# Between the last attention heads and the output projection: one store for both parts of a head's output, the last half's norm one part sooner, scratch cut per 256 tokens, and the products that are ready first put first

## The chip, the cores and the metric

The kernel runs on one core of one Trainium2 chip. A core has a matrix engine (TensorE, "PE" in the profile, with its weight loads as "PEld"), a vector engine (VectorE, "DVE"), a scalar engine (ScalarE, "ACT"), a third elementwise engine (GpSimd, "POOL"), and SyncE ("SP"), which here issues all transfers between the on-chip memory and device memory. Each engine takes its instructions in program order and waits on semaphores of the others. The metric is the device time of one execution in microseconds.

## What is computed

Two layers of a decoder over 1024 tokens of width 1024, in float32. The part that matters here is each layer's attention and the output projection behind it:

```python
# layer 0: 8 FoX heads and 8 MLA heads of width 64, their outputs side by side
m = jnp.concatenate([fox_out, mla_out], axis=-1) @ w_out      # 1024 x 1024
# layer 1: 8 differential heads of width 128, each normed over its width
o = _rms_norm(o, subln) * (1.0 - lambda_init)
m = o.reshape(bsz, seq, ODD_MIX_WIDTH) @ w_out
# both layers
x = x + _rms_norm(m, norm_mix_post[layer])
h = _rms_norm(x, norm_ffn_pre[layer])
f = _conv_ffn(h, ffn_w_up[layer], ffn_conv_w[layer], ffn_conv_b[layer], ffn_w_down[layer])
x = x + _rms_norm(f, norm_ffn_post[layer])
```

## The kernel before

**Products.** Every float32 product is made of three matrix products: a value is split into a high part `h`, rounded to the format that PE reads, and a low part `l = x - h`; `mm3` (L143) issues high x high, high x low and low x high into one PSUM bank. So each operand is made twice on the elementwise engines: ACT casts the high part and DVE or POOL subtracts (`split`, L121 and L122).

**Order.** The kernel is written in a tile framework that puts the instructions of each engine in order by a simulated timeline, and gives out buffers by tag: `Q` and `WL` hold 2 KB per partition each, `o` has two buffers, `h` and `l` one each (the tiles `oso`, `osh`, `osl`). Whatever changes a wait or a buffer can move instructions anywhere in the stages around it. Generators are woven: the scores and pv products of a head are mixed with dense products (weights, the first half of the output projection).

**Heads of layer 0.** A head goes through four parts of 256 query rows, j = 3, 2, 1, 0. `p_transpose` turns the probabilities (PE L385, then the cast to `pt`/`ptq` on ACT L389 and the subtraction on DVE L390). `pv64` multiplies them with V, whose high and low parts stand side by side in 128 columns, so that rows 0 to 63 and 64 to 127 of the bank `pspv` are to be added: ACT copies one half to `o` (L412), DVE adds the other (L413), ACT casts `h` (L414), POOL subtracts `l` (L415), and SP stores both to the scratch `oT` in device memory (L417, L418). It runs 64 times.

**Heads of layer 1.** `diff_head` makes parts of 256 rows too, and norms halves of 512 rows, i.e. two parts. `sub_a` squares a half (ACT L1175), sums the squares on PE (L1177) and takes the reciprocal root on DVE, sixteen small operations of 128 x 4 one behind the other (L172 to L179, then L1182 and L1183). `sub_b` spreads the result over the rows through diagonal matrices (L1192, L1193, PE L1195 and L1196), scales (DVE L1198), splits and stores (L1202, L1203), for c = 0 and 1, 256 tokens each. Both are put in a list (`pend`) and called one part later each: half 1, complete after j = 2, has its `sub_a` called at j = 1 and its `sub_b` at j = 0.

**Output projection.** `out_first` multiplies heads 0 to 3 (k 0 to 3) into the first 512 columns while the heads still run. `out_second` does the rest for blocks of 128 tokens, m = 7 down to 0: `ot` is the transposed head output, loaded by `oT_load` from the scratch (SP L442), kg = 0 for k 0 to 3 and kg = 1 for k 4 to 7. For each m, bank `psS` gets k 4 to 7 of the first 512 columns (n = 0, 12 matmuls) and bank `psmm` all eight k of the last 512 (n = 1, 24 matmuls). What follows an m on DVE, ACT and POOL is the post-norm, the residual sum and the pre-norm of the feed-forward part; SP also loads the residual rows `xr` (L198).

## Time and profile before

| | us |
|---|---|
| three runs, median | 2580.59 |
| lowest and highest of them | 2574.98, 2582.19 |
| the profiled execution, its own time | 2578.5 |
| its span, first to last instruction | 2576.4 |

The mean granted clock of TensorE in it is 0.977. The page gives for each engine its busy time, the share of the span and the number of instructions; a row of a timeline gives start, duration, engine, line, operation, output and inputs, shape, count, and in brackets the idle time before it with what ended that. The names are those of the program. The stages that the change touches lie in the profile as follows.

| stage | us from the span's start |
|---|---|
| layer 0, heads | about 110 to 564 |
| layer 0, first product of `out_second` behind the heads | 570.6 |
| layer 1, last product of the last head's part 2 | 1814.7 |
| layer 1, first product of `out_second` behind the heads | 1831.1 |

### The profile page before, as it was taken

The page shows a single profiled execution, that of the slowest core. Times are in us where ns is not written, and L with a number is a line of the kernel's source. Part 1 is how long each engine was busy: PE and PEld are TensorE (multiplying, and loading weights), DVE is VectorE, ACT ScalarE, POOL GpSimd, SP SyncE. Part 2 cuts the span into 40 slices and gives each one's busy share as a digit, 9 for nine tenths or more (in the row PEclk, how much of TensorE's full clock was granted, in tenths as well). Part 3 has the DMA queues.
Part 4 walks back from the last instruction along what each step waited for, and adds up shares of the span by engine and source line. Part 5 has one row for each costly group of instructions (what it writes and reads, how often), then busy time and mean ns, then how long its engine had stood idle before and what let it go on. Part 6 is the DMA issues. An engine that isn't in the chain of part 4 may idle for free.

```text
span 2576.4 us, 36603 instructions
## 1 busy us (share of the span) xinstructions
PE 2457.8 (95%) x12326; PEld 2072.2 (80%) x12326; DVE 1754.5 (68%) x3615; ACT 1232.3 (48%) x2457; POOL 1256.7 (49%) x1140
## 2 busy tenths in 40 slices
PE   9999899989899999989999999999889999999898
PEld 7888788868688888868888888888768888887786
DVE  5556788758766665666876777678687656656668
ACT  4455578654433333434545555456453333334353
POOL 3445665444577777740421323222257777776122
PEclk9999999999899999999999999999899999999899
DMA  3232333355223323584432213133732332328545
GB/s 142 86 99 80 105 90 88 105 163 189 73 94 112 109 93 112 182 276 151 164 136 58 70 49 88 34 107 107 237 115 88 105 106 98 107 102 278 169 150 192
DMA packets 189531, 316.16 MB, mean 123 GB/s; under 512 B 17928, under 2 KB 85144, under 8 KB 189344
## 3 DMA queue, kind: packets, MB, share of 16 engines
q1 hardware_dynamic: 189344, 313.83, 37.5%
q8 instruction: 98, 1.61, 0.3%
q14 instruction: 89, 0.73, 0.1%
HBM read 222.23 MB, written 76.85 MB: 116 GB/s over the span
## 4 chain that ended last, share of the span: by engine, by line
PE 38%; DVE 5%; DMA 2%; POOL 2%; issue 2%; ACT 1%; SPq 0%; DVEq 0%; POOLq 0%; ACTq 0%
PE psmm L143 19%; PE psS L143 6%; PE pstr L143 6%; PE pspv L143 5%; PE pstr L385 1%; DVE d L122 1%; DMA wdside<-in_ffn_down_dram 0%; DMA dB<-in_ffn_down_dram 0%; PE pstr L1177 0%; POOL d L122 0%; DVE xq L222 0%; DVE t L348 0%; DVE dT L726 0%; DVE xq L221 0%; DVE t L1230 0%
## 5 line engine op out<-in xcount | busy, mean ns | idle before, releaser
L143 PE MATMUL psmm<-hT,whi 128*128 128x512 f32 (+1 forms) x960 | 309.9, 399 | 2.3 <-DVE qb L320 2.3
L356 ACT ACTIVATE t<-t,mn 128x896 f32<-128x896 f32 (+7 forms) x256 | 198.8, 777 | 126.1 <-DVE mn L348 114.8
L122 POOL TENSOR_TENSOR wlo<-wraw,whi 128x512 fp32r<-128x512 f32 (+2 forms) x96 | 129.5, 1358 | 260.0 <-ACT whi L121 234.9
L122 POOL TENSOR_TENSOR d<-uraw,d 128x512 fp32r<-128x512 f32 x66 | 103.8, 1593 | 215.5 <-ACT d L121 209.5
L143 PEld LDWEIGHTS psmm<-hT,whi 128*128 128x128 f32 (+1 forms) x960 | 174.0, 188 | 35.9 <-issue 2.5
L143 PE MATMUL psmm<-hT,wlo 128*128 128x512 f32 (+1 forms) x480 | 189.4, 395 | 0.8 <-POOL wlo L122 0.8
L121 ACT CAST d<-uraw 128x512 fp32r<-128x512 f32 x154 | 91.8, 618 | 139.8 <-DMA uraw<-uS 67.9
L385 PE MATMUL pstr<-ident,t 128*128 128x128 f32 x864 | 136.4, 281 | 7.6 <-DVE t L1230 3.1
L143 PE MATMUL psmm<-whi,hT 128*128 128x256 f32 (+1 forms) x576 | 123.6, 303 | 5.4 <-DVE hT L253 2.8
L143 PE MATMUL psmm<-wo,ot 128*128 128x512 f32 x448 | 123.7, 396 | 0.0
L385 PEld LDWEIGHTS pstr<-ident,t 128*128 128x128 f32 x864 | 103.5, 145 | 17.9 <-DVE t L1230 3.7
L630 ACT ACTIVATE y<-y,cols 128x1024 f32<-128x1024 f32 x44 | 50.7, 1152 | 138.4 <-DVE y L628 138.4
L143 PE MATMUL pstr<-T,S3h 128*128 128x512 f32 x352 | 112.1, 399 | 3.8 <-DVE B L523 3.8
L626 ACT ACTIVATE y<-gate,cols 128x1024 f32<-128x1024 f32 x44 | 50.8, 1155 | 130.7 <-DVE gate L621 130.7
L143 PE MATMUL psmm<-B,A12h 128*128 128x512 f32 x352 | 109.0, 390 | 2.1 <-DVE B L523 2.1
L143 PE MATMUL psmm<-B,A11h 128*128 128x512 f32 x352 | 109.4, 390 | 0.0
L143 PE MATMUL pstr<-T,A22h 128*128 128x512 f32 x352 | 108.7, 389 | 0.0
L143 PE MATMUL psmm<-T,S2h 128*128 128x512 f32 x352 | 108.4, 389 | 0.0
L122 DVE TENSOR_TENSOR S2l<-s,S2h 128x512 fp32r<-128x512 f32 x44 | 56.7, 1289 | 74.8 <-ACT S2h L121 74.8
L143 PEld LDWEIGHTS psmm<-hT,wlo 128*128 128x128 f32 (+1 forms) x480 | 90.1, 188 | 20.8 <-POOL wlo L122 1.0
L390 DVE TENSOR_TENSOR ptq<-pstr,ptq 128x512 fp32r<-128x512 f32 (+1 forms) x160 | 99.4, 629 | 10.3 <-ACT ptq L389 7.9
L143 PE MATMUL psS<-B,S4h 128*128 128x512 f32 x336 | 103.7, 390 | 1.1 <-ACT S4h L121 1.1
(362 smaller groups left out, 7540.5 us busy)
## 6 DMA issues: line engine op xcount, KB each, us to landing
ot<-oT SPq DMA_DIRECT2D x96, 256.0 KB, 3.8
wg<-in_ffn_up_dram SPq DMA_DIRECT2D x44, 512.0 KB, 3.5
wv<-in_ffn_up_dram SPq DMA_DIRECT2D x44, 512.0 KB, 3.5
uS<-us SPq DMA_DIRECT2D x88, 256.0 KB, 2.0
uraw<-uS SPq DMA_DIRECT2D x40, 512.0 KB, 4.1
uA<-y SPq DMA_DIRECT2D x66, 256.0 KB, 2.1
wdside<-in_ffn_down_dram SPq DMA_DIRECT2D x66, 256.0 KB, 4.8
uraw<-uA SPq DMA_DIRECT2D x30, 512.0 KB, 4.3
```

The lines of the kernel that those rows point to most:

```text
L121: nc.scalar.copy(R(hi), raw)
L122: return lo_eng.tensor_tensor(R(lo), raw, hi, ALU.subtract).ins
L143: ins = nc.tensor.matmul(out, R(l), R(r), start=first and j == 0, stop=last and j == n - 1, skip_group_check=more).ins
L356: nc.scalar.activation(t[:, :W], t[:, :W], AF.Exp, bias=mn, scale=-1.0, accum_out=l)
L385: nc.tensor.transpose(tp[:, c:c + P], pts[qi][:, b * P:(b + 1) * P], ident)
L390: nc.vector.tensor_tensor(R(pl[:, :c]), tp[:, :c], ph[:, :c], ALU.subtract)
L626: nc.scalar.activation(y, gp, AF.Copy, scale=col(2, f))
L630: nc.scalar.activation(y, y, AF.Gelu_apprx_tanh, bias=cb)
```

## The change

There are five edits. (1) The scratch `oT_d` is cut into one tile for each layer, kg and part j, so that a load waits for the stores of its own 256 tokens and heads. (2) `pv64` always puts its sum in partitions 0 to 63, writes the high part to partitions 0 to 63 and the low part to 64 to 127 of one buffer, and stores both with one transfer; the buffer alternates between the tags `h` and `l`; the subtraction is an operation of DVE (`scalar_tensor_tensor`) in place of POOL's. (3) In `out_second`, the load for m = 7 of kg = 0 takes its buffers from `WL`; m = 7 and m = 6 do n = 1 before n = 0, and m = 6 begins n = 1 with k 0 to 3, as m = 7 did already. (4) `sub_b` does c = 1 first and leaves the low part where the sum stood, in `osub`. (5) For the last head, `sub_a` of half 1 is called as soon as part j = 2 is done, which brings its `sub_b` to j = 1.

```diff
@@ -111,7 +111,8 @@
     kr_d = dr.tile([2, 32, S], F32, tag="kr_d", name="kr_d")
     cr_d = dr.tile([2, S], F32, tag="cr_d", name="cr_d")
     ck_d = dr.tile([8, S], F32, tag="ck_d", name="ck_d")
-    oT_d = [dr.tile([2, 8, P, S], F32, tag=f"oT{i}", name=f"oT{i}") for i in range(2)]
+
+    oT_d = [[[dr.tile([2, 4, P, 256], F32, tag=f"oT{i}{kg}{j}", name=f"oT{i}{kg}{j}") for j in range(4)] for kg in range(2)] for i in range(2)]
     u_d = [{n: dr.tile([NP, P, HALF], F32, tag=f"u{n}{i}", name=f"u{n}{i}") for n in ("A11", "A12", "A22", "S1", "S2", "S3", "S4")}
            for i in range(2)]
 
@@ -395,6 +396,8 @@
             out.append((b, ph[:, c0:c0 + n], pl[:, c0:c0 + n], qi * P))
         return out
 
+    stg = [0]
+
     def pv64(pts, i0, vcols, up, oT, k, done):
 
         ov = bank("pv", 256)
@@ -405,17 +408,15 @@
                 done += (256 - c0) / 9216
             if kb + 2 < nb:
                 yield done
-        a0, b0 = (64, 0) if up else (0, 64)
+
         o = ostage("o", bufs=2)
-        h, l = ostage("h"), ostage("l")
-        ra, rb = slice(a0, a0 + 64), slice(b0, b0 + 64)
-        nc.scalar.copy(o[ra], ov[rb])
-        nc.vector.tensor_tensor(o[ra], ov[ra], o[ra], ALU.add)
-        nc.scalar.copy(R(h[ra]), o[ra])
-        nc.gpsimd.tensor_tensor(R(l[ra]), o[ra], h[ra], ALU.subtract)
-        qs = slice(i0 * P, i0 * P + 256)
-        nc.sync.dma_start(oT[0, k, ra, qs], h[ra])
-        nc.sync.dma_start(oT[1, k, ra, qs], l[ra])
+        stg[0] ^= 1
+        hl_ = ostage("hl"[stg[0]])
+        nc.scalar.copy(o[0:64], ov[64:128])
+        nc.vector.tensor_tensor(o[0:64], ov[0:64], o[0:64], ALU.add)
+        nc.scalar.copy(R(hl_[0:64]), o[0:64])
+        nc.vector.scalar_tensor_tensor(R(hl_[64:128]), o[0:64], 1.0, hl_[0:64], ALU.mult, ALU.subtract)
+        nc.sync.dma_start(oT[k // 4][i0 // 2][:, k % 4, 64 * up:64 * up + 64, :], hl_)
         yield done
         return done
 
@@ -440,7 +441,7 @@
         for j in range(2):
             t = buf(tag, "ot")
             nc.sync.dma_start(t.rearrange("p (k c) -> p k c", k=4),
-                              oT[j, 4 * kg:4 * kg + 4, :, m * P:(m + 1) * P].rearrange("k p c -> p k c"))
+                              oT[kg][m // 2][j, :, :, (m % 2) * P:(m % 2 + 1) * P].rearrange("k p c -> p k c"))
             ts.append(t)
         return ts
 
@@ -469,7 +470,7 @@
 
         lo = buf("X", "wo")
         w1 = wo_load(w_src, 0, 1, lambda k: (buf("Q", "woh"), lo[:, k, :]))
-        o1 = {7: oT_load(oT, 0, 7, "Q")}
+        o1 = {7: oT_load(oT, 0, 7)}
         w0 = wo_load(w_src, 4, 0, lambda k: (buf("Q", "woh"), buf("Q", "wol")))
         w1 += wo_quads(w_src, 4, 1)
         ot = {m: oT_load(oT, 1, m) for m in (7, 6, 5)}
@@ -482,10 +483,10 @@
                 o1[m - 1] = oT_load(oT, 0, m - 1, "Q")
             if m:
                 fin_0(m - 1)
-            rows = []
-            for n in range(2):
+            rows = {}
+            for n in (1, 0) if m > 5 else (0, 1):
                 o = bank("S" if n == 0 else "mm")
-                ks = ((4, 5, 6, 7) if n == 0 else (0, 1, 2, 3, 4, 5, 6, 7) if m == 7 else (4, 5, 6, 7, 0, 1, 2, 3))
+                ks = ((4, 5, 6, 7) if n == 0 else (0, 1, 2, 3, 4, 5, 6, 7) if m > 5 else (4, 5, 6, 7, 0, 1, 2, 3))
                 for k in ks:
                     src = (ot if k > 3 else o1)[m]
                     mm3(o, hl(tuple(t[:, (k % 4) * P:(k % 4 + 1) * P] for t in src), w0[k - 4] if n == 0 else w1[k]), k == ks[0], k == ks[-1])
@@ -495,7 +496,7 @@
                     fin_e(m, 0, r)
                 else:
                     r = o
-                rows.append(r)
+                rows[n] = r
             fin_a(m, 1, rows[1], rows[0])
             if m < 7:
                 fin_b(m + 1)
@@ -1185,7 +1186,7 @@
 
     def sub_b(h, half, o, rh, rl):
         eng = nc.vector if h == 7 and LV else nc.gpsimd
-        for c in range(2):
+        for c in (1, 0):
             dh, dl = ostage("h"), ostage("l")
             for m in range(2):
                 ms, mc = slice(m * P, (m + 1) * P), slice(2 * c + m, 2 * c + m + 1)
@@ -1196,11 +1197,11 @@
             nc.tensor.matmul(rb, ones_r, R(dl), start=False, stop=True)
             oc = o[:, c * 256:(c + 1) * 256]
             nc.vector.scalar_tensor_tensor(oc, oc, subg, rb, ALU.mult, ALU.mult)
-            oh, ol = ostage("o", bufs=2), ostage("o", bufs=2)
-            split(oc, oh, ol, eng)
-            qs = slice(half * HALF + c * 256, half * HALF + (c + 1) * 256)
-            nc.sync.dma_start(oT_d[1][0, h, :, qs], oh)
-            nc.sync.dma_start(oT_d[1][1, h, :, qs], ol)
+            oh = ostage("o", bufs=2)
+            split(oc, oh, oc, eng)
+            od = oT_d[1][h // 4][2 * half + c]
+            nc.sync.dma_start(od[0, h % 4], oh)
+            nc.sync.dma_start(od[1, h % 4], oc)
 
     def diff_head(h, maps, V, pend):
 
@@ -1247,6 +1248,8 @@
             nc.scalar.copy(o[:, (j % 2) * 256:(j % 2 + 1) * 256], ov)
             if j % 2 == 0:
                 pend.append(lambda h=h, j=j, o=o, l1=l1: sub_a(h, j // 2, o, l1))
+                if h == 7 and j == 2:
+                    pend.append(pend.pop(0)())
             yield done
 
     values, maps = diff_v(0, VT), diff_qk(0)
```

Lines of the changed kernel are higher by one from L115 on, by three from L400 on until `pv64`'s end and by one behind it (L143 is L144, L442 is L443, L1195 is L1196). Three places show how the order of the instructions moves.

PE at the end of layer 0's heads, before the change. `pspv` is the bank of a part of the last head, `ot_7039` the high part of heads 4 to 7 for m = 7:

```order
L143 MATMUL pspv_6903<-ptq_713,Vm_4308 128x256 x2
L143 MATMUL pspv_6903<-ptq_713,Vm_4308 128x128 x2
L143 MATMUL pspv_6958<-ptq_713,Vm_4308 128x256 x2
L143 MATMUL pspv_6958<-ptq_713,Vm_4308 128x128 x2
L143 MATMUL psS_7065<-woh_7007,ot_7039 128x512
L143 MATMUL psS_7065<-wol_7008,ot_7039 128x512
L143 MATMUL psmm_7082<-wo_7025,ot_7039 128x512
```

So PE goes from the last pv (`pspv_6958`, part 0) straight to k 4 to 7 of m = 7. With the change, PE ahead of the last head's first pv; `ot_6937` and `ot_6939` are the high and low parts of heads 0 to 3 for m = 6:

```order
L386 MATMUL pstr_6676<-ident,t_6606 128x128
L386 MATMUL pstr_6676<-ident,t_6624 128x128 x2
L144 MATMUL psmm_7030<-woh_6873,ot_6937 128x512
L144 MATMUL psmm_7030<-wo_6870,ot_6937 128x512
L144 MATMUL psmm_7030<-woh_6873,ot_6939 128x512
L144 MATMUL psmm_7030<-woh_6876,ot_6937 128x512
L144 MATMUL psmm_7030<-wo_6870,ot_6937 128x512
```

And PE at the last head's end with the change; `ot_6925` is the high part of heads 4 to 7 for m = 7:

```order
L144 MATMUL pspv_6793<-ptq_727,Vm_4258 128x256 x2
L144 MATMUL pspv_6793<-ptq_727,Vm_4258 128x128 x2
L144 MATMUL pspv_6846<-ptq_727,Vm_4258 128x256 x2
L144 MATMUL pspv_6846<-ptq_727,Vm_4258 128x128 x2
L144 MATMUL psmm_6951<-wo_6911,ot_6925 128x512
L144 MATMUL psmm_6951<-wo_6912,ot_6925 128x512
L144 MATMUL psS_6976<-woh_6893,ot_6925 128x512
```

The twelve products of m = 6 with k 0 to 3 (five of them shown) have moved from behind the heads to a place ahead of the last head's pv. Behind the last pv, m = 7 begins with n = 1.

SP at the same place, before; `oT_100` is the whole scratch, the stores write there from `osh` and `osl`, and `ot_7039` and `ot_7041` are m = 7:

```order
L198 DMA xr_7055<-in_x_dram 128x1024
L198 DMA xr_7062<-in_x_dram 128x1024
L417 DMA oT_100<-osh_6793 64x256
L418 DMA oT_100<-osl_6794 64x256
L182 DMA gain_6978<-in_g_mix_post_dram 128x512
L182 DMA gain_6980<-in_g_mix_post_dram 128x512
L442 DMA ot_7039<-oT_100 128x4x128
L442 DMA ot_7041<-oT_100 128x4x128
```

And SP with the change; `oT_107` and `oT_106` are the scratch of heads 4 to 7 for parts 3 and 2, `ot_6925` and `ot_6927` are m = 7:

```order
L199 DMA xr_6941<-in_x_dram 128x1024
L199 DMA xr_6948<-in_x_dram 128x1024
L419 DMA oT_107<-osl_6687 2x64x256
L183 DMA gain_6864<-in_g_mix_post_dram 128x512
L419 DMA oT_106<-osh_6763 2x64x256
L183 DMA gain_6866<-in_g_mix_post_dram 128x512
L443 DMA ot_6925<-oT_107 128x4x128
L443 DMA ot_6927<-oT_107 128x4x128
```

Before, the loads of m = 7 stand behind the two stores of part 3. With the change they stand behind one store of part 3 and one of part 2; the residual rows are ahead of both as before.

PE at the end of layer 1's last head, before; `psS_19693` is m = 7, `pspv_19426` and `pspv_19529` are parts 1 and 0, L1177 is the sums of squares of `sub_a`, L1195 and L1196 are the products of `sub_b`:

```order
L143 MATMUL pspv_19426<-pt_13847,vd_17238 128x128
L1195 MATMUL pstr_19503<-osh_19497,ones 128x256
L1196 MATMUL pstr_19503<-osl_19498,ones 128x256
L1195 MATMUL pstr_19519<-osh_19513,ones 128x256
L385 MATMUL pstr_19530<-ident,t_19453 128x128
L385 MATMUL pstr_19530<-ident,t_19475 128x128 x2
L1196 MATMUL pstr_19519<-osl_19514,ones 128x256
L143 MATMUL pspv_19529<-ptq_13849,vd_17238 128x256 x3
L143 MATMUL pspv_19529<-ptq_13849,vd_17238 128x128 x3
L1177 MATMUL pstr_19543<-ones,osh_19544 128x1 x2
L1177 MATMUL pstr_19543<-ones,osl_19548 128x1 x2
L143 MATMUL psS_19693<-woh_19635,ot_19667 128x512
```

And with the change, from the end of part 2 (`pspv_19140`) on; L1178, L1196 and L1197 are the same three lines, L386 the transposes of part 1:

```order
L144 MATMUL pspv_19140<-ptq_13735,vd_17435 128x128 x3
L1178 MATMUL pstr_19198<-ones,osh_19199 128x1 x2
L1178 MATMUL pstr_19198<-ones,osl_19203 128x1 x2
L1196 MATMUL pstr_19290<-osh_19284,ones 128x256
L1197 MATMUL pstr_19290<-osl_19285,ones 128x256
L1196 MATMUL pstr_19305<-osh_19299,ones 128x256
L386 MATMUL pstr_19315<-ident,t_19233 128x128
L386 MATMUL pstr_19315<-ident,t_19258 128x128
L386 MATMUL pstr_19315<-ident,t_19233 128x128
L386 MATMUL pstr_19315<-ident,t_19258 128x128
L386 MATMUL pstr_19328<-ident,t_19233 128x128
```

`sub_b` of half 1 stood behind part 1's products and now stands directly behind `sub_a`, ahead of part 1's transposes. Half 0's moves the other way: its last matmuls stood among the products of m = 6, and with the change the row before the first product of m = 3 is the last of them.

## Prediction

> **What bounds the kernel now.** I read the head of the page first, then the windows by stage, then the timelines of the two places where the last heads meet the output projection.
>
> ```profile
> span 2576.4 us, 36603 instructions
> PE 2457.8 (95%) x12326; PEld 2072.2 (80%) x12326; DVE 1754.5 (68%) x3615; ACT 1232.3 (48%) x2457; POOL 1256.7 (49%) x1140
> ```
>
> PE is busy for 2457.8 of 2576.4 us, and the change takes no product away. So it can win only PE's idle time and the slow clock behind it: 118.6 us idle over the whole span, of which the change reaches three places. The first is the attention of layer 0 (110 to 564 us; columns: length, then the busy time of PE, PEld, DVE, ACT and POOL):
>
> ```profile
> sum 454.00, PE 427.10 PEld 369.21 DVE 321.61 ACT 302.64 POOL 249.65; mean PE 106.78 PEld 92.30 DVE 80.40 ACT 75.66 POOL 62.41
> ```
>
> PE idles 454.0 - 427.1 = 26.9 us there, in many small waits. The second is the hand-over from the last MLA head to the projection:
>
> ```profile
> 557.00:564.00 7.00, 4.76 (x36) 3.93 (x35) 3.93 (x8) 3.70 (x9) 1.97 (x4) 1.00 0.98 309
> 564.00:571.00 7.00, 0.83 (x4) 0.72 (x5) 0.75 (x2) 0.77 (x2) 0.72 (x1) 0.53 0.75 262
> ```
>
> The last three columns are granted clock, DMA share and GB/s. PE works 0.83 of the 7 us from 564 on. Its timeline shows the wait:
>
> ```profile
> 570.62 0.77 PE L143 MATMUL psS<-woh,ot 128*128 128x512 f32 x1 [6.17 <-DMA ot<-oT]
> ...
> 574.60 0.44 PE L143 MATMUL psS<-wol,ot 128*128 128x512 f32 x1
> ...
> 580.80 2.88 PE L143 MATMUL psmm<-wo,ot 128*128 128x512 f32 x12
> 583.52 0.39 PE L143 MATMUL psmm<-woh,ot 128*128 128x512 f32 x1
> ```
>
> Twelve products take 583.52 - 580.80 = 2.72 us, 0.227 us each. The nine from 570.62 to 574.60 take 3.98 us where they should take 2.04: the gap of 6.17 us costs 1.94 us more in clock. The third place is the same hand-over in layer 1:
>
> ```profile
> 1815.00:1831.00 16.00, 11.34 (x48) 9.32 (x48) 9.04 (x40) 4.28 (x11) 0.73 (x1) 0.57 0.73 252
> ```
>
> Here PE idles 16 - 11.34 = 4.7 us and runs at 0.57 of its clock: a chain of small steps, not PE, sets the time.
>
> **Term 1, layer 0: twelve products ahead of the last head's end.** The k 0 to 3 products of m = 6 now stand on PE in front of the last head's first pv. After the head, m = 7 and m = 6 have twelve products less to do, 12 x 0.227 = **-2.7 us**, if m = 7's last four heads arrive when they did. The twelve themselves fall into the 2.24 us that PE idles in 557 to 564 and the 6.17 us behind it; should they push the head, they push work that ends before the load does.
>
> **Term 2, layer 0: when m = 7's load can go.** SP's timeline and the store's landing, measured from its issue:
>
> ```profile
> 558.66 0.89 SPq L198 DMA_DIRECT2D xr<-in_x_dram  x2
> 561.02 0.45 SPq L417 DMA_DIRECT2D oT<-osh  x1
> ...
> 567.59 2.02 SPq L442 DMA_DIRECT2D ot<-oT  x4
> ```
>
> ```profile
> DMA to landing us min/median/max: 6.5/6.5/6.5
> ```
>
> ```profile
> DMA to landing us min/median/max: 1.9/2.0/6.5
> ```
>
> ```profile
> DMA to landing us min/median/max: 2.9/3.8/4.6
> ```
>
> The first answer is the hi store of 561.02: it lands at 567.5, and the load goes at 567.59. The second is all 64 hi stores: 2.0 us as a rule. The third is the four loads of 567.59. This one is slow because 1 MB of residual rows was issued just before it, with the DMA share at 0.98. What makes its issue late is seen on ACT, and the add between on DVE:
>
> ```profile
> 557.31 0.36 ACT L412 COPY oso<-pspv 64x256 f32<-64x256 f32 x1
> ...
> 560.59 0.40 ACT L414 CAST osh<-oso 64x256 fp32r<-64x256 f32 x1 [2.42 <-DMA oT<-osh]
> ...
> 562.01 0.36 ACT L412 COPY oso<-pspv 64x256 f32<-64x256 f32 x1
> ```
>
> ```profile
> 558.04 0.43 DVE L413 TENSOR_TENSOR oso<-pspv,oso 64x256 f32<-64x256 f32 x1
> ```
>
> With two buffers the 2.42 us wait for the buffer goes, and with the difference on DVE instead of POOL the store could be issued at 558.47 + 0.40 + 0.42 = 559.3, earlier by 1.7 us, less what the twelve products delay the pv before it. But the residual rows still stand ahead of it on SP, and with two more Q buffers two more 256 KB loads of heads 0 to 3 run earlier, 0.5 MB or 1.7 us at 309 GB/s. If the queue must drain first, the landing stays at 567.5 (late end: +1.7). If the landing follows the issue by 2.0 us, the next limit is SP's order: m = 7's loads now stand behind the store of the head's second part too, whose copy starts at 562.01 on ACT now and whose store could go 1.6 us later (copy, add, cast, difference), near 564; the load lands 2.9 us behind, near 567.3 instead of 570.6: -3.3, and with a gap this short the 1.94 us of clock as well (early end: -5.2). I take **0**, since the 0.98 is the nearest row.
>
> The Trainium skill ("DMA: Bandwidth & Descriptors", section "Queues, rings and completion order") says that each DMA engine takes its descriptors in ring order and that the semaphore's write lands after all earlier writes of that engine. By it this term is 0 or worse; by the 2.0 us row it would be -5.2. The 6.5 us above agrees with the page.
>
> **Term 3, layer 0: the subtraction moves from POOL to DVE.**
>
> ```profile
> L413 DVE TENSOR_TENSOR oso<-pspv,oso x64: 398/422/429, 122.3 to 569.3; 64x256 f32<-64x256 f32 x64
> ```
>
> ```profile
> L415 POOL TENSOR_TENSOR osl<-oso,osh x64: 718/732/1053, 124.9 to 579.4; 64x256 fp32r<-64x256 f32 x64
> ```
>
> POOL loses 64 x 0.73 = 47 us. DVE gets 64 operations of the add's shape, 64 x 0.42 = 27 us on 322: 8% more. What PE waits for there, in 320 to 564 and in 110 to 320 (us in total, times, longest):
>
> ```profile
> PE psS L143 <- DVE mn L348: 3.9, 3, 2.7
> ...
> PE pstr L385 <- DVE pt L390: 0.5, 1, 0.5
> ```
>
> ```profile
> PE pspv L143 <- DVE ptq L390: 2.1, 2, 1.7
> PE pstr L385 <- POOL t L933: 1.6, 2, 1.1
> ...
> PE psS L143 <- DVE oso L413: 0.7, 1, 0.7
> ```
>
> The seven DVE rows of the first answer and the six of the second, of which the first and the last stand here, come to 11.0 and 7.7 us; 8% of them is +1.5. POOL's 1.6 us, with a fifth of its load gone, is -0.3. Ends: -2.3 (the waits for POOL and for the add vanish, 1.6 + 0.7) to +4 (some ten of the 64 stand right behind their add on DVE and stall it for the 0.40 us cast, all of it reaching PE). I take **+1.2**. The 64 issues less on SP cost and bring nothing that a wait shows. Splitting the scratch moves no byte; the in-place low part saves a buffer and adds a wait only on a buffer two parts later.
>
> **Term 4, layer 1: the norm of half 1 begins before part 1.**
>
> ```profile
> 1813.87 0.81 PE L143 MATMUL pspv<-ptq,vd 128*128 128x256 f32 x6
> 1815.58 0.61 PE L1177 MATMUL pstr<-ones,osh 128*128 128x1 f32 x4 [0.91 <-ACT osh L1175]
> ...
> 1816.50 1.16 PE L385 MATMUL pstr<-ident,t 128*128 128x128 f32 x7
> ...
> 1822.03 0.54 PE L1196 MATMUL pstr<-osl,ones 128*128 128x256 f32 x1
> ...
> 1831.11 0.79 PE L143 MATMUL psS<-woh,ot 128*128 128x512 f32 x1 [1.65 <-DMA ot<-oT]
> ```
>
> ```profile
> 1821.06 0.48 DVE L1192 TENSOR_SCALAR osh<-ident,rhl 128x128 fp32r<-128x128 f32 x2
> ...
> 1829.49 0.16 DVE L172 SCALAR_TENSOR_TENSOR rv<-pstr,l 128x4 f32<-128x4 f32 x1 [2.63 <-PE pstr L1177]
> ...
> 1832.76 0.48 DVE L1192 TENSOR_SCALAR osh<-ident,rhl 128x128 fp32r<-128x128 f32 x2
> ```
>
> ```profile
> 1823.61 2.29 DMA oT<-oso
> 1826.43 1.77 DMA oT<-oso
> 1828.21 2.85 DMA ot<-oT
> ...
> 1853.35 0.87 PE pstr L240 x8
> ```
>
> The last fence is the chain of waits: m = 7 starts after the second hi store (1826.43), its landing and the load. Now the part that m = 7 needs (c = 1) is first. Twelve products of m = 6 push part 2's end from 1814.7 to 1817.4; ACT's wait and L1177, as now, to 1819.2, and 0.2 (an estimate) until DVE has it; the norm chain alone 1832.76 - 1829.49 = 3.3 to 1822.7; from L1192 to the store as now (1821.06 to 1823.61) 2.6, so 1825.2; landing 1.77, load 2.85: m = 7 starts at 1829.9, **-1.2**. PE waits about 3 us for the norm chain with part 1 queued behind it; part 1 then fills the wait for the load. From the start on there are twelve products less (-2.7), but part 0's pv (0.8) and half 0's sums (1816.50 - 1815.58 = 0.9) now come after it: -1.0. Together **-2.2**.
>
> **Term 5, layer 1: a new wait at m = 3.** Half 0's last part moves back to m = 4, and m = 3's first product, four microseconds behind it on PE, needs its store and load. Between them stand 16 products and 8 transposes: 16 x 0.227 + 0.87 = 4.5 us. The chain is 1823.61 - 1822.03 = 1.6 to the store, 2.29 landing, 2.85 load: 6.7. **+2.2**; ends 0 (the norm chain runs ahead) and +9 (below).
>
> Sum: -2.7 + 0 + 1.2 - 2.2 + 2.2 = **-1.5**. The profiled execution takes 2578.5 us (span 2576.4 and 2.1 around it), 2.1 less than the median 2580.6. That gives 2577.0 by the one, 2579.1 by the other; I say **2578**, midway, and count the rivals from there.
>
> **Rivals.** (a) Early landing: term 2 at its early end, term 3 at 0, m = 3 without a wait: -2.7 - 5.2 - 2.2 = -10.1, 8.6 below the forecast, **2569**. For it speaks the 2.42 us wait that goes; against it the share of 0.98. Half-way stands a shorter gap alone: the Trainium skill ("TensorE: Matmul & The Clock Gate", "Part 1: The HAM clock gate") halves the clock after an idle window of about 3.4 us. In rows, that is: should the 6.17 us gap become so short, the 1.94 us are saved and nothing else, 2576, chance 0.1. The row of 0.53 behind the long gap agrees with the page; no run here yet shows a short one.
>
> (b) Nothing gained: the twelve products delay the last head, its store and so m = 7 by the 2.7 us they save, since PE works on the head all the time they take: term 1 is 0, **2581**. For it: they stand in front of all four of its parts. Against it: PE idles 2.24 of the 7 us there.
>
> (c) Slower: m = 3's wait grows, because its store and load go through full queues.
>
> ```profile
> 1850.00:1860.00 10.00, 10.00 (x50) 8.35 (x49) 7.79 (x22) 4.75 (x12) 2.88 (x2) 1.00 0.99 311
> ```
>
> The stage has a DMA share of 0.99 and DVE busy 7.79 of 10. With the store at 6.5 us, as in layer 0, +4.2; the load at 4.6 (the longest of those of 567.59) +1.7; DVE's 0.9 us in the chain at a free share of 0.22 +3.2: 9.1 more than the forecast, **2587**, 7.6 slower than before. It decides from a chain of 6.7 + 1.5 = 8.2 us on. Against it: PE has 59 products, 13 us, between half 0's sums and this part.
>
> **Chances and range.** The forecast (2572 to 2584) 0.40; the shorter gap 0.10; (a) 0.22; (b) 0.15; (c) 0.13. About 0.3% (7.7 us) can be told from no change: that is 2572.9 and 2588.3. Faster takes (a) and a little of the forecast, 0.26; slower half of (c) and a tail, 0.09; same 0.65. The range leaves out the ends of (a) and (c): 2566 to 2588.
>
> **What will show it.** Term 1: m = 6's twelve products before the last head's pv, and m = 7 still starting some 3 us after its load at about 567.5. Term 2: the merged store's time to landing, 5 us and more or near 2. Term 3: DVE busy up by 27 us in 110 to 564, POOL down by 47, PE idle 27 to 29. Term 4: m = 7 in layer 1 starting about 10 us after the end of part 1's transposes, PE idle 3 us before L1192's consumer. Term 5: PE waiting some 2 us for a load at m = 3. Wrong it would be if PE idles much more in the attention of either layer, whose order moves throughout.

## The result, and the profile after

The change makes the kernel slower: 2598.91 us median of 4 runs (2596.14 to 2602.60) against 2580.24 us of the kernel before, a ratio of 1.0069 [1.0055, 1.0084]. The forecast was 2578 with a range to 2588, so both the value and the sign were wrong. Four of the kernels below (`u_l1`, `a_l1`, `a_wide`, `w_l1`) had one much slower run each, which is left out of their ratios and medians. The profiled execution took 2600.5 us, with a span of 2598.4, 22.0 more than before.

The head of the page after the change:

```profile
span 2598.4 us, 36539 instructions
PE 2464.9 (95%) x12326; PEld 2075.6 (80%) x12326; DVE 1789.3 (69%) x3679; ACT 1230.8 (47%) x2457; POOL 1208.3 (46%) x1076
```

PE does the same 12326 instructions and is busy only 7.1 us longer, so 14.9 of the 22.0 us are new idle time. DVE has 34.8 us more and POOL 48.4 less. PE is still the busiest, at 95%.

To see where the time went I cut both traces at the end of the last head's pv in layer 0 and at ACT's first gelu row of the first FFN. Before, on PE and then on ACT:

```profile
563.90 0.56 PE L143 MATMUL pspv<-ptq,Vm 128*128 128x256 f32 x3 [0.33 <-DVE ptq L390]
```

```profile
683.16 1.16 ACT L626 ACTIVATE y<-gate,cols 128x1024 f32<-128x1024 f32 x1 [8.86 <-DVE gate L621]
```

After, the same two places, with PE's first product of the projection:

```profile
581.64 0.68 PE L144 MATMUL pspv<-ptq,Vm 128*128 128x256 f32 x4 [0.22 <-DVE ptq L391]
595.83 1.22 PE L144 MATMUL psmm<-wo,ot 128*128 128x512 f32 x2 [13.51 <-DMA ot<-oT]
```

```profile
707.10 1.15 ACT L627 ACTIVATE y<-gate,cols 128x1024 f32<-128x1024 f32 x1 [7.31 <-DVE gate L622]
```

The heads end at 582.3 instead of 564.5, 17.8 later, of which the twelve products put in front of the last head account for 2.7. The stretch from there to the first gelu row takes 124.8 instead of 118.7, 6.1 longer, though it has those twelve products less. All the rest, layer 1 with its two edits included, is 1.9 us shorter. The loss is in layer 0, and most of it falls before the end of the last head, at a place that the forecast priced at a few waits for DVE.

The windows of the stages after the change (length, then busy PE, PEld, DVE, ACT and POOL, then granted clock, DMA share, GB/s):

```profile
110.00:582.30 472.30, 438.66 (x2571) 378.06 (x2569) 350.04 (x1024) 301.75 (x684) 207.24 (x274) 0.97 0.32 95
...
582.30:595.80 13.50, 0.02 (x1) 0.00 (x0) 2.09 (x5) 1.95 (x5) 0.00 (x0) 0.65 0.64 213
595.80:606.00 10.20, 10.17 (x36) 8.25 (x37) 1.60 (x4) 2.43 (x5) 0.95 (x1) 0.80 0.55 166
```

The heads before, in the same columns:

```profile
110.00:564.00 454.00, 427.10 (x2555) 369.21 (x2553) 321.61 (x962) 302.64 (x684) 249.65 (x335) 0.99 0.35 99
```

PE idles 33.6 us in the heads (26.9 before). It is also busy 11.6 us longer: 2.7 by the twelve products, and the other 8.9, some 2%, for the same work at a granted clock of 0.97 instead of 0.99. The gap ahead of the projection is 13.5 us against 6.2. The slice behind it runs at 0.80, as it did before (570.6 to 580.8), so the longer gap costs no more clock than the shorter one.

What the stores do on the DMA engines shows where a pv64 store stands alone, at its first part in layer 0. SP's issue before, then 40 slices of 0.175 us from 123 on, the busy share of the 16 DMA engines in tenths and what they moved:

```profile
123.53 0.47 SPq L417 DMA_DIRECT2D oT<-osh  x1
```

```profile
DMA  0000000103920000000001850000009756979995
GB/s 0 0 0 0 0 0 0 47 0 94 217 65 0 0 0 0 0 0 0 0 0 41 211 117 6 0 0 0 0 0 140 117 94 234 328 304 445 421 398 164
```

The high part is a burst of three slices (94, 217 and 65 GB/s by 0.175 us are 66 KB); the low part follows as a second one. The same place after the change, from 124 on:

```profile
124.50 0.59 SPq L419 DMA_DIRECT2D oT<-osl  x1
```

```profile
DMA  0000100000101111111111111142349899699324
GB/s 0 0 0 0 47 0 0 0 0 12 35 23 53 47 18 41 35 47 18 41 29 53 47 47 47 47 140 94 111 117 281 328 398 374 164 351 281 70 117 187
```

The merged store is no burst: the share stands at about 0.1 for sixteen slices, 2.8 us, at 12 to 53 GB/s. That is 110 of its 131 KB; the rest goes on under the next burst. A share of 0.1 fits two of sixteen engines (0.125): the transfer's outermost dimension is the pair of parts, 2 by 64 rows by 256 columns. The count of packets on the page says the same; before and after:

```profile
DMA packets 189531, 316.16 MB, mean 123 GB/s; under 512 B 17928, under 2 KB 85144, under 8 KB 189344
```

```profile
DMA packets 187611, 316.16 MB, mean 122 GB/s; under 512 B 16008, under 2 KB 83224, under 8 KB 187424
```

The bytes are the same, and 1920 packets under 512 B are gone, 30 for each of the 64 calls of `pv64`. That is what two stores that post 16 completions each leave when one with 2 takes their place (32 - 2). The Trainium skill ("DMA: Bandwidth & Descriptors", section "Why a DMA increments its semaphore by 16 and not by 1", at "How many engines") states this: the number of engines is the largest one up to 16 that divides the outermost dimension of both sides, and only those engines post a completion. By it the old stores (64 rows) use 16 and the new one 2; the trace agrees with both, by the 0.1 and by the 1920.

**Two places where it is paid.** First the passage from the FoX heads to the MLA heads. After the change, SP's issues, and ACT and PE behind them:

```profile
314.76 0.55 SPq L419 DMA_DIRECT2D oT<-osl  x1
315.76 0.32 SPq L962 DMA_DIRECT2D craw<-cn_d  x1
316.20 8.24 SPq L128 DMA_DIRECT2D wraw<-in_uq_dram  x2
...
322.19 0.51 ACT L122 CAST whi<-wraw 128x384 fp32r<-128x384 f32 x1 [3.73 <-DMA wraw<-in_uq_dram]
322.75 0.73 PE L144 MATMUL psmm<-cq,whi 128*128 128x512 f32 x2 [2.75 <-ACT whi L122]
```

```profile
DMA  0000000129757999952111011000001000001767
```

The second fence has slices of 0.3 us from 314 on. The row of 316.20 joins two issues; the second goes at about 324. The first one's weights reach ACT at 322.19, 6.0 us after the issue; before, these loads land in 2.6 us:

```profile
wraw<-in_uq_dram SPq DMA_DIRECT2D x6, 192.0 KB, 2.6
```

The share is at 0.9 until about 319, and then 0.1 to 0.2 until 321.5. I read this so: fourteen engines have finished their part of the two loads (`craw`, 512 KB, and the first of the weights, 192 KB), and the two that still carry the store of 314.76 have theirs behind it. That is a reading of one place: `craw` is ahead of the weights too and has its share in the 6.0 us. The first scores of the MLA heads come at 376.2 instead of 365.1, 11.1 of the 17.8 us.

The second place is the end of the last head. SP's queue after the change, and its wait from 586 to 592 (total, times, longest):

```profile
580.80 0.49 SPq L419 DMA_DIRECT2D oT<-osl  x1
581.40 2.99 SPq L183 DMA_DIRECT2D gain<-in_g_mix_post_dram  x1
585.07 0.49 SPq L419 DMA_DIRECT2D oT<-osh  x1
585.66 3.07 SPq L183 DMA_DIRECT2D gain<-in_g_mix_post_dram  x1
591.02 6.24 SPq L443 DMA_DIRECT2D ot<-oT  x8
```

```profile
SPq L443 <- DMA oT<-osl: 2.2, 1, 2.2
```

The load goes when the store of 580.80 has landed, 10.2 us after its issue; before, it went 6.6 behind the store of 561.02. So the gap's growth (13.51 - 6.17 = 7.3) adds up: landing +3.6; the store is issued 1.5 us ahead of the last pv's end instead of 3.4, +1.9; and the load takes 4.8 us until PE starts (591.02 to 595.83) instead of 3.0, +1.8.

### The profile page after: what moved, and what is told of

The parts are those of the page before. It is cut to its first block, busy times and chain, and to the rows that moved or that the text cites. A ratio compares the mean times of both kernels' runs of the same rounds, so it can differ in the third digit from the quotient of the medians.

```text
span 2598.4 us, 36539 instructions
## 1 busy us (share of the span) xinstructions
PE 2464.9 (95%) x12326; PEld 2075.6 (80%) x12326; DVE 1789.3 (69%) x3679; ACT 1230.8 (47%) x2457; POOL 1208.3 (46%) x1076
## 5 line engine op out<-in xcount | busy, mean ns | idle before, releaser
L144 PE MATMUL psmm<-hT,whi 128*128 128x512 f32 (+1 forms) x960 | 308.2, 397 | 0.6 <-DVE qb L321 0.6
L144 PEld LDWEIGHTS psmm<-hT,whi 128*128 128x128 f32 (+1 forms) x960 | 173.2, 187 | 32.8 <-issue 0.8
L144 PE MATMUL psmm<-hT,wlo 128*128 128x512 f32 (+1 forms) x480 | 188.7, 393 | 0.0
L386 PE MATMUL pstr<-ident,t 128*128 128x128 f32 x864 | 136.9, 280 | 16.0 <-DVE pt L391 4.0
L144 PE MATMUL psmm<-wo,ot 128*128 128x512 f32 x448 | 127.8, 404 | 16.0 <-DMA ot<-oT 16.0
L386 PEld LDWEIGHTS pstr<-ident,t 128*128 128x128 f32 x864 | 103.3, 144 | 28.3 <-POOL t L934 5.0
L144 PE MATMUL psmm<-whi,hT 128*128 128x256 f32 (+1 forms) x576 | 121.7, 300 | 4.0 <-DVE hT L254 2.8
L144 PE MATMUL pstr<-T,S3h 128*128 128x512 f32 x352 | 111.6, 398 | 2.5 <-ACT S3h L122 2.3
L144 PE MATMUL psmm<-B,A12h 128*128 128x512 f32 x352 | 110.0, 393 | 2.5 <-DVE B L524 2.5
L391 DVE TENSOR_TENSOR ptq<-pstr,ptq 128x512 fp32r<-128x512 f32 (+1 forms) x160 | 99.8, 630 | 17.7 <-ACT ptq L390 15.7
L620 DVE TENSOR_TENSOR u<-u,psmm 128x512 f32<-128x512 f32 x44 | 30.0, 681 | 117.3 <-PE psmm L144 117.3
L144 PEld LDWEIGHTS psmm<-wo,ot 128*128 128x128 f32 x448 | 84.7, 195 | 32.6 <-DMA ot<-oT 16.3
L144 PE MATMUL psmm<-B,A11h 128*128 128x512 f32 x352 | 109.4, 390 | 0.0
L144 PE MATMUL pstr<-T,A22h 128*128 128x512 f32 x352 | 108.7, 389 | 0.0
L144 PE MATMUL psmm<-T,S2h 128*128 128x512 f32 x352 | 108.5, 389 | 0.0
```

The source lines that it names most:

```text
L144: ins = nc.tensor.matmul(out, R(l), R(r), start=first and j == 0, stop=last and j == n - 1, skip_group_check=more).ins
L386: nc.tensor.transpose(tp[:, c:c + P], pts[qi][:, b * P:(b + 1) * P], ident)
L391: nc.vector.tensor_tensor(R(pl[:, :c]), tp[:, :c], ph[:, :c], ALU.subtract)
L620: nc.vector.tensor_tensor(u2, s1, p6, ALU.add)
```

## The experiments

Ratios are to the kernel before, run on the same chip, with a 95% interval. Theories are named by letters. In the first group S says that the subtraction, now on DVE, comes late and holds SP's store; T puts the loss on the new order of `out_second`; R says that any edit shuffles the order of the heads and costs something. In the second, D is DVE's extra work and Q is SP's queue, held by one store that needs both parts. E, from the third on, is the two engines.

**Which part.** Three kernels are the change without one part, and one has part 1 alone.

`u_pv`: the change without part 2. Against the kernel before, its `pv64` differs only in where it stores:

```diff
-        qs = slice(i0 * P, i0 * P + 256)
-        nc.sync.dma_start(oT[0, k, ra, qs], h[ra])
-        nc.sync.dma_start(oT[1, k, ra, qs], l[ra])
+        od = oT[k // 4][i0 // 2]
+        nc.sync.dma_start(od[0, k % 4, ra], h[ra])
+        nc.sync.dma_start(od[1, k % 4, ra], l[ra])
```

> The change without its part (2): pv64 as before (two buffers, POOL's subtraction, two stores), scratch cut, the rest of the change kept. Theory S (the subtraction on DVE comes late, so the one store comes late, and SP, which works in order, holds back the loads queued behind it): the heads of layer 0 lose their 15 us again and m = 7 in layer 0 waits about 6 us for its load instead of 13.5; about 2577 us. Theory T (the order and the buffers of out_second cause it): stays at 2595 to 2600. Theory R (any edit shuffles the whole order by chance): anywhere from 2570 to 2600, with the loss at other places.

Measured 2583.96, 1.0019 [1.0001, 1.0036].

`u_os`: the change without part 3 (`out_second` as before).

> The change without its part (3): out_second as before (Q buffers, n = 0 first, only m = 7 with k 0 to 3 first). Theory S: the heads of layer 0 stay 15 us late, only the products ahead of the last head go (-3 us there, +3 behind): 2595 to 2602. Theory T: the loss of the heads and of the load goes, about 2578. Theory R: anywhere, with other places.

Measured 2598.15, 1.0069 [1.0042, 1.0097].

`u_l1`: the change without parts 4 and 5.

> The change without its parts (4) and (5): sub_b and diff_head as before. If the in-place low part and the order of sub_b give layer 1's heads the 15 us that the trace shows as won there, and cost its hand-over the 10 us that it shows as lost, those two go and the rest stays: about 2604. If they come from the shuffle (theory R), layer 1 may differ in any way; layer 0 stays as in the change (2 us at most) in every theory but R.

Measured 2597.32, 1.0065 [1.0040, 1.0091].

`a_split`: the kernel before with part 1 alone.

> The kernel before with part (1) alone: the scratch cut, same stores, same loads, same engines. Theories S and T: nothing but waits on fewer stores, 2578 to 2582. Theory R: moves by 5 us or more, since the order is made anew.

Measured 2581.15, 1.0000 [0.9989, 1.0012]. The loss goes with part 2: without it 0.19% is left of 0.69. T falls, and so does R as the main cause, since the edits of `u_pv` move the order as well. (`a_split` does not test R: in its trace every engine has the order of before.)

**What in part 2.** `a_pv` is the kernel before with part 2 alone.

> The kernel before with part (2) alone: 64 subtractions on DVE, one buffer, one store, whole scratch. If part (2) is the cause by itself: 2592 to 2600. If it costs only together with the order of out_second: 2580 to 2586.

Measured 2600.08, 1.0061 [1.0041, 1.0081]. Part 2 does it by itself. The next three take it apart. `pvpool` puts the subtraction back on POOL:

```diff
-        nc.vector.scalar_tensor_tensor(R(hl_[64:128]), o[0:64], 1.0, hl_[0:64], ALU.mult, ALU.subtract)
+        nc.gpsimd.tensor_tensor(R(hl_[64:128]), o[0:64], hl_[0:64], ALU.subtract)
```

> The change with the subtraction of part (2) on POOL again; one buffer, one store and all other parts as in the change. Theory D (the subtraction waits in DVE's queue and adds 27 us to it): most of the 15 us that part (2) costs come back, 2580 to 2586. Theory Q (SP is held by one store that waits for the low part, whoever makes it): little comes back, 2592 to 2600.

Measured 2597.27, 1.0059 [1.0039, 1.0079]. `pv2` keeps DVE and the new buffer, and stores the two halves apart:

```diff
+        od = oT[k // 4][i0 // 2]
         nc.vector.scalar_tensor_tensor(R(hl_[64:128]), o[0:64], 1.0, hl_[0:64], ALU.mult, ALU.subtract)
-        nc.sync.dma_start(oT[k // 4][i0 // 2][:, k % 4, 64 * up:64 * up + 64, :], hl_)
+        nc.sync.dma_start(od[0, k % 4, 64 * up:64 * up + 64, :], hl_[0:64])
+        nc.sync.dma_start(od[1, k % 4, 64 * up:64 * up + 64, :], hl_[64:128])
```

> The change with two stores for each call in place of one (high part, then low part), the subtraction still on DVE. Theory D: 2594 to 2602. Theory Q in its narrow form (merging the stores makes SP wait longer): back to 2580 to 2586; in its wide form (SP waits for the low part in any case): as in the change.

Measured 2585.53, 1.0021 [1.0006, 1.0037]. `pvact` issues the merged store from ACT's queue:

```diff
-        nc.sync.dma_start(oT[k // 4][i0 // 2][:, k % 4, 64 * up:64 * up + 64, :], hl_)
+        nc.scalar.dma_start(oT[k // 4][i0 // 2][:, k % 4, 64 * up:64 * up + 64, :], hl_)
```

> The change with the store of part (2) issued by ACT's queue in place of SP's; the subtraction still on DVE. Theory Q: SP no longer waits for the low part, the loads behind it go in time, the gap at 319 to 323 us (SP's wait of 9.0 us for the low part, PE's of 2.75 for a weight) closes and about 15 us come back: 2580 to 2586, unless ACT, which now waits for DVE in its place, loses as much. Theory D: 2594 to 2604.

Measured 2594.38, 1.0044 [1.0031, 1.0057]. S and D fall with the first two: the engine of the subtraction does not matter, the merging does. `pv2` fits Q as well, in its narrow form. The third speaks against Q as the whole story, since with SP free of the store most of the loss stays. Its gap ahead of the projection is still long:

```profile
586.22 1.22 PE L143 MATMUL psmm<-wo,ot 128*128 128x512 f32 x2 [11.07 <-DMA ot<-oT]
```

**Two engines, or one store.** `wide1` is the change with one merged store as well, but with the parts side by side in 64 partitions, so that its outermost dimension is 64. One buffer serves in place of two. (The cast and the subtraction, left out here, write the two halves of its columns.)

```diff
-        hl_ = ostage("hl"[stg[0]])
+        hl_ = ostage("w", 512)
...
-        nc.sync.dma_start(oT[k // 4][i0 // 2][:, k % 4, 64 * up:64 * up + 64, :], hl_)
+        nc.sync.dma_start(oT[k // 4][i0 // 2][:, k % 4, 64 * up:64 * up + 64, :].rearrange("j p c -> p j c"), hl_[0:64].rearrange("p (j c) -> p j c", j=2))
```

> The change with its one store kept, but the two parts side by side in 64 partitions of one 512-column buffer, so that the slowest dimension of the store is 64; one such buffer in place of two. Theory E: the loss of the merged store goes, 2580 to 2588, up to 4 us more for the single buffer. Theory Q: stays at 2594 to 2602, since SP still waits for both parts.

Measured 2582.45, 1.0000 [0.9990, 1.0010]. The whole loss is gone. Its first store alone, slices of 0.175 us from 123 on, and its packets:

```profile
DMA  0000000001000007995000000000000000648999
GB/s 0 0 0 0 0 0 0 0 0 47 0 0 0 0 0 181 217 217 123 12 0 0 0 0 0 0 0 0 0 0 0 0 0 0 140 140 304 374 421 445
```

```profile
DMA packets 188505, 316.14 MB, mean 122 GB/s; under 512 B 16904, under 2 KB 84120, under 8 KB 188320
```

131 KB go in five slices, 0.9 us, at a share up to 0.9. The packets are 1026 fewer than before, and 64 x 16 = 1024 is what one store with 16 completions in place of two makes. Q needs one store to be bad; here is one store, issued when both parts are ready, and over the whole kernel it is not. At the hand-over it is not free, though:

```profile
573.75 1.22 PE L143 MATMUL psmm<-wo,ot 128*128 128x512 f32 x2 [9.46 <-DMA ot<-oT]
```

With one buffer, ACT waits 4.56 us until 567.52 for the store of 560.43 to land, SP's next store goes at 568.40, and the load of m = 7 stands behind it. So the change's gap of 13.5 us is not the two engines alone. Nor is a gap exact to a microsecond: in `a_l1`, whose order in layer 0 is that of before, it is 7.52 (6.17 before).

`a_two` was to do the opposite: the kernel before, with its stores' rows written as two groups of 32.

```diff
-        nc.sync.dma_start(oT[0, k, ra, qs], h[ra])
-        nc.sync.dma_start(oT[1, k, ra, qs], l[ra])
+        nc.sync.dma_start(oT[0, k, ra, qs].rearrange("(a p) c -> a p c", a=2), h[ra])
+        nc.sync.dma_start(oT[1, k, ra, qs].rearrange("(a p) c -> a p c", a=2), l[ra])
```

> The kernel before; only the target of its two stores is written with the 64 rows as 2 x 32, so that the slowest dimension is 2, as in the merged store. Same bytes, same engines, the same order of instructions on every engine. Theory E (such a store runs on 2 of the 16 DMA engines, and its rows and everything queued behind them on those two come late): 2592 to 2602, DMA share 0.1 while a store runs alone, heads of layer 0 some 15 us longer. Theory Q (SP waits longer because one store needs both parts): 2578 to 2583, as before.

Measured 2580.44, 1.0001 [0.9992, 1.0010], and **inconclusive**: its packets are the 189531 of before. Two groups of 32 rows with one stride throughout are one run of 64 rows, and the store went out as such. `a_perm` mends that: even rows as one group, odd rows as the other, which cannot be joined. This permutes the rows of the scratch, so its output is not the right one. It is otherwise the kernel before, with the same number of stores, the same sizes and, in the trace, the same order on every engine, so that neither R nor Q has a place in it.

```diff
-        nc.sync.dma_start(oT[0, k, ra, qs], h[ra])
-        nc.sync.dma_start(oT[1, k, ra, qs], l[ra])
+        nc.sync.dma_start(oT[0, k, ra, qs].rearrange("(p a) c -> a p c", a=2), h[ra])
+        nc.sync.dma_start(oT[1, k, ra, qs].rearrange("(p a) c -> a p c", a=2), l[ra])
```

> The kernel before with its two stores' 64 rows written as 2 x 32 in a form that can't be merged back into 64 (even rows, then odd ones, so that the rows of the scratch are permuted and the output isn't the reference's). Bytes, engines and the order on every engine are those of before. Theory E (2 of 16 DMA engines): DMA share 0.1 while a store runs alone, fewer packets by 128 x 14 = 1792 (2 completions in place of 16 for each store), and 2592 to 2602. Theory Q (SP's wait for both parts): 2578 to 2583, since nothing is merged.

Measured 2595.57, 1.0061 [1.0048, 1.0074]. Its first store alone, slices as above, and its packets:

```profile
DMA  0000010001011111100011011114936799887553
GB/s 0 0 0 0 0 47 0 18 12 18 23 47 47 47 53 47 47 18 0 18 18 12 23 47 53 47 47 140 211 88 211 281 374 304 234 304 211 211 187 141
```

```profile
DMA packets 187739, 316.16 MB, mean 122 GB/s; under 512 B 16136, under 2 KB 83352, under 8 KB 187552
```

The share of 0.1 is back, now for both stores, and 1792 packets are gone: 128 stores by 14. With nothing of the change in it, the outermost dimension of 2 alone costs 0.61%, most of the change's 0.69. Its heads end at 579.4 (564.5 before), with the clock and idle time of the change:

```profile
110.00:579.40 469.40, 434.96 (x2555) 375.49 (x2553) 321.31 (x960) 302.96 (x684) 249.69 (x334) 0.97 0.32 96
```

The way from the slow store to PE is not the same in the two kernels. In the heads of `a_perm` most of the new waits are for the buffers that the stores read: POOL waits 34.4 us until a low part has landed (3.4 before) and ACT 9.3 for a high part (3.2). In the heads of the change ACT waits 15.1 us for the weights' loads (6.3 before, 3.8 in `wide1`). So `a_perm` shows what the shape can cost here, not that the change pays it by the same path.

**What the rest of the change is worth.** With the store in its 64-row form, or as before, the other parts can be measured.

`a_os`: the kernel before with part 3 alone.

> The kernel before with part (3) alone (load of m = 7 from WL, n = 1 first for m = 7 and 6, k 0 to 3 first for m = 6). By term 1 as forecast: -2.7 us in each layer, 2574 to 2577. If the products gained are given back because DVE's norm chain or the slow clock sets the end of the projection: 2579 to 2583.

Measured 2583.18, 1.0009 [1.0000, 1.0019].

`a_l1`: the kernel before with parts 4 and 5 alone.

> The kernel before with parts (4) and (5) alone (c = 1 first, low part in place, sub_b of half 1 one part sooner). By terms 4 and 5 as forecast, without the twelve products: the start of m = 7 some 4 us sooner, a new wait of 0 to 2 us later: 2577 to 2580. If PE's wait for the norm chain with part 1 behind it outweighs it: 2582 to 2587.

Measured 2581.26, 1.0000 [0.9990, 1.0009].

`a_wide`: the kernel before with parts 1 and 2, the store with 64 rows.

> The kernel before with part (1) and part (2) alone, part (2) in the form whose slowest dimension is 64 (parts side by side in one 512-column buffer). Theory E: what part (2) was meant to bring, without its cost: 2576 to 2583. Theory Q: 2594 to 2602.

Measured 2581.35, 0.9999 [0.9990, 1.0008].

`w_l1`: the change without part 3, the store with 64 rows.

> The change without part (3), part (2) in the 64-row form. If part (3) is what costs the 2 to 3 us that it cost alone: 2577 to 2581. If parts (4) and (5) cost as much in layer 1's hand-over: 2582 to 2587.

Measured 2580.49, 0.9991 [0.9980, 1.0003].

`w_os`: the change without parts 4 and 5, the store with 64 rows.

> The change without parts (4) and (5), part (2) in the 64-row form. If part (3) costs 2 to 3 us here too: 2582 to 2586. If it needs the earlier store of part (2) to gain: 2573 to 2579.

Measured 2580.75, 1.0002 [0.9992, 1.0011]. None of them is clearly apart from the kernel before; `a_os` stands at the edge. `w_os` falls between the two ranges expected of it, and `a_l1` between its two as well, so these two decide nothing. `w_l1` has the lowest ratio, and its interval holds 1; no version here is shown to beat the kernel before.

## Why the prediction was wrong, step by step

**The step that failed** is in terms 2 and 3: the merged store was costed like the two old ones. "Splitting the scratch moves no byte" and "The 64 issues less on SP cost and bring nothing that a wait shows" speak of bytes and of SP, but the trace was not asked how many DMA engines a store uses, and the outermost dimension went from 64 to 2. A lone store's slices, at a share up to 0.9 before, would have raised the question. No term held a cost for it in the heads; the shape alone costs +15.7 us by `a_perm` (0.61% [0.48, 0.74] of 2580). In the heads, PE idles 33.6 us after the change and 34.4 in `a_perm`, where term 3 expected 27 to 29, and the same work takes some 8 to 9 us longer at a granted clock of 0.97. Neither end of the range and no rival held it. The prediction's last sign of being wrong, PE idling much more in the attention of a layer, is the one that came true. Rival (c) had the right sign with another mechanism at another place, and what it priced did not occur.

**Term 1 (-2.7)** was forecast at its place and given back behind it. The twelve products stand before the last pv; with the old stores (`u_pv`) m = 7 starts when it did (570.64 against 570.62):

```profile
570.64 1.22 PE L143 MATMUL psmm<-wo,ot 128*128 128x512 f32 x2 [5.54 <-DMA ot<-oT]
573.59 3.96 PE L143 MATMUL psmm<-wo,ot 128*128 128x512 f32 x10 [0.88 <-DMA ot<-oT]
...
642.75 0.50 PE L143 MATMUL psmm<-woh,ot 128*128 128x512 f32 x1 [2.11 <-DMA ot<-oT]
644.69 1.09 PE L143 MATMUL psmm<-woh,ot 128*128 128x512 f32 x2 [1.21 <-DMA ot<-oT]
```

Waits for these loads come to 5.54 + 0.88 + 2.11 + 1.21 = 9.7 us; before it was 6.17 and one more of 0.16. The 3.4 us more take the 2.7 back, and this is no accident of one profile: these waits add up to between 6.05 and 8.25 us in the six profiles without part 3 and without stores of two groups (`before`, `a_l1`, `a_two`, `a_split`, `a_wide`, `w_l1`), and to between 9.74 and 11.76 in the five with part 3 (`a_os`, `u_pv`, `pv2`, `wide1`, `w_os`). One of them, some 70 us behind the start of m = 7, is 2.0 to 2.1 us in all five and at most 0.7 in the six. The projection's products were the cover for later loads, and with fewer of them the loads are late. From the last pv to the first gelu row it takes 119.5 us in `u_pv`, 118.7 before. In `a_os`:

```profile
572.51 1.22 PE L143 MATMUL psmm<-wo,ot 128*128 128x512 f32 x2 [7.55 <-DMA ot<-oT]
575.62 4.64 PE L143 MATMUL psmm<-wo,ot 128*128 128x512 f32 x10 [1.04 <-DMA ot<-oT]
```

Its gap of 7.55 is no more than `a_l1` has without part 3 (7.52), so that is not put down to the part. Ten products take 4.64 us there and 3.96 in `u_pv`, against 2.43 for a row of ten later in both (580.34 and 583.68): with a gap of 5.54 us, the shortest ahead of this projection in any run, the slow clock is still paid, so the rival of a shorter gap was not met. This comes to rival (b)'s 0, by another way than it said; by `a_os` the part is worth +2.3 us, between 0 and 4.9 by its interval.

**Term 2 (0)** holds where the store is not merged, as `u_pv` shows. For the change I had named "5 us and more or near 2" as the test, and the store that m = 7 waits for took 10.2. The page of the changed kernel gives no time to landing for any transfer, so the sign that I had asked for could be read only from SP's wait. The ring-order rule of the Trainium skill that the prediction weighed here allowed "0 or worse"; worse it was. In `wide1` the store with 64 rows has landed after 7.1 us (560.43 to ACT's cast at 567.52). By these two profiles some 3 of the 10.2 us go with the shape, and the rest is near the 6.5 of the store before.

**Term 3 (+1.2)** was a small term and is not the cause. In `wide1`, which differs from the change only in the store and its buffer, the heads read:

```profile
110.00:564.30 454.30, 429.86 (x2570) 370.28 (x2569) 341.10 (x1023) 301.83 (x683) 208.80 (x274) 0.99 0.35 100
```

POOL is down by 40.9 us and DVE up by 19.5 (forecast 47 and 27), and PE idles 454.3 - 429.9 = 24.4 us, 2.5 less than before and not 1.2 more; the twelve products in it may fill some of the waits. That DVE's work reaches PE isn't shown anywhere, and `pvpool` and the change cannot be told apart.

**Terms 4 (-2.2) and 5 (+2.2)** stand in layer 1, whose stores are not merged. On PE after the change:

```profile
1824.28 0.50 PE L144 MATMUL psmm<-woh,ot 128*128 128x512 f32 x1 [1.25 <-DMA ot<-oT]
1831.98 0.61 PE L1178 MATMUL pstr<-ones,osh 128*128 128x1 f32 x4 [0.91 <-ACT osh L1176]
1837.03 0.55 PE L1196 MATMUL pstr<-osh,ones 128*128 128x256 f32 x1 [4.00 <-DVE osh L1193]
...
1845.90 1.22 PE L144 MATMUL psmm<-wo,ot 128*128 128x512 f32 x2 [2.47 <-DMA ot<-oT]
...
1878.92 0.50 PE L144 MATMUL psS<-woh,ot 128*128 128x512 f32 x1 [0.98 <-DMA ot<-oT]
```

Part 2 ends at 1831.98 - 0.91 = 1831.07, and m = 7 starts 14.8 us later; the forecast was 12.5 (1817.4 to 1829.9), and it was 16.4 before (1814.7 to 1831.1). So the order of steps is right, with a norm wait of 4.00 instead of 3, and a load that PE still awaits for 2.47. The moved products, meant to fill time, waited for a load of their own (1.25). The new wait at m = 3 is there and has 0.98 us, not 2.2. The two terms were to cancel, and `a_l1` gives 1.0000 [0.9990, 1.0009]: that agrees, but a pair of terms of 2 us each cannot be tested apart by it.

**What stays open.** `u_pv` and `pv2` are 0.2% slower than before with intervals that end close above 1, while `wide1` is at 1.0000 with the same other parts. I did not find what in them costs 4 us. That the store on ACT's queue (`pvact`) brings part of the loss back is measured (1.0044 against 1.0069, with intervals that just touch), its way not traced. The loss in the heads was followed at one place only, not store by store. And in `a_perm` the rows of a group also lie at twice the stride, which no run takes apart; the change itself loses as much without that.

## What to carry to other kernels

When two transfers are joined into one, look at the outermost dimension of the joined shape, not only at its bytes and its issues: a pair put outside turned a transfer of sixteen DMA engines into one of two, and what waited were loads behind it in the change and the buffers that it read in `a_perm`. Keep the long dimension outside (partitions first, the pair inside), and check it in the trace where a transfer stands alone, by the DMA share and by the count of packets. And products that are moved ahead to shorten a stage can be missed there as cover for its loads.

## What the runs showed of the hardware that was not expected

- A store of 2 x 64 x 256 had moved 110 of its 131 KB after 2.8 us at a DMA share of 0.1; the same bytes as 64 x 2 x 256 take 0.9 us at up to 0.9 (`wide1`). With 64 such stores this kernel was 0.7% slower, though the DMA engines are busy only a third of the time in that stage (0.32).
- Groups of rows that lie at one stride are one dimension to the transfer: written as 2 x 32 they changed nothing (`a_two`, 1.0001), and with even and odd rows apart they cost 0.61% (`a_perm`). So it isn't the way the code writes a shape that counts, but whether its dimensions can be joined.
- A load of 192 KB behind such a store and a load of 512 KB took 6.0 us instead of 2.6. That the store on two engines held back its last part is read from the DMA share there, and not shown by a run.
